# A hybrid decoder layer's opening: rows, first projections, two gates and operand sums emitted in an order that an event simulation of four engines finds

## The chip, the cores and the metric

The kernel runs on one core of one Trainium2 chip. A core has TensorE (PE, matrix products), VectorE (DVE), ScalarE (ACT), GpSimd (POOL) and SyncE (SP, which only issues transfers here); each takes its own instructions in order and waits on semaphores for the others. The metric is the device time of one execution in microseconds (us); lower is better.

## The reference

The whole is one decoder layer in float32 on 1024 tokens of width 1024. What the change touches is the first part, up to the projections:

```
h    = rms_norm(x, norm1_g)              # per token: x * rsqrt(mean(x*x) + 1e-6) * g
proj = h @ w_in + b_in                   # 1024 x D_IN, split by columns into
# qa ka va fa | qb kb vb | qc kc vc ksl vsl kwn vwn gc | gates (3 x 1024)
y_a = fox_attention(qa, ka, va, fa)      # c = cumsum(log_sigmoid(fa)) forgets along the keys
y_b = dilated_attention(qb, kb, vb)
y_c = nsa_attention(qc, ..., gc)
merged = sum(sigmoid(gates[:, i]) * (y_i @ w_i))
x = x + merged @ w_o;  x = x + conv_ffn(rms_norm(x, norm2_g));  return rms_norm(x, final_g)
```

The order in which the parts of `proj` are computed is free. The attention, the merge and the feed-forward part follow on the same core.

## The kernel before

**Numbers.** Every large product is made of three: an operand is split into a rounded high part (ACT, a cast or copy) and a low part, the difference (DVE or POOL, a subtraction with two inputs in SBUF). `mm3` (L294 to L299) issues high x high, high x low, low x high. So each weight and each activation costs one ACT and one DVE or POOL instruction before PE can use it.

**Rows.** `start` (L337 on) loads the eight 128-token rows of x and, after the second, the first token weights. `phase0` (L424) takes row by row: mean square (ACT), a Newton step for the inverse root on DVE (`rstd`, L314 to L324), the scaling x (L428, DVE), two times four transposes by PE into the banks T and S (L433), then the high part hTh (ACT, L436) and the low part hTl (DVE, L437). `constants2` transposes biases and converts masks.

**First tokens.** `proj_va` multiplies each of the eight token blocks with 260 columns (va and fa): 24 matmuls of 260 columns into one of two banks dn. The evacuation tm (L692, DVE) adds the bias and frees the bank; fa (L714) is copied out; v is cast by ACT (L703), its low part made by POOL (L704), and stored. The weights' split bh, bl comes in four chunks (L668 on ACT, L669 on POOL), and the raw chunks go through two buffers wr, so that the third load waits for the first split.

**Gates.** `gate(0)` and `gate(1)` each make two products of 24 matmuls of 512 columns, one per half of the tokens, also into the banks dn. Their weights wl are split by POOL, one instruction of 1024 elements (L275). The evacuation f is an ACT instruction (L1441) and frees the bank, and the result dg is stored from ACT's queue.

**Second tokens.** `proj_vn` does with 274 columns what `proj_va` does with 260, its weights split by POOL (L669).

**Sums.** `token_sums` (L471 on) prepares the operands of a Strassen-like scheme for the later pair products: for each of four slices i it forms T1 (three DVE additions, L488 to L490), T2 (two, L493 and L494), T3 (two, L497 and L498) and T4 (two on POOL, L499 and L501), and splits each (ACT L485; the low part, L486, of T1 and T3 on DVE, of T2 and T4 on POOL). Its steps stand between the tokens and the gates in the program (`step`).

**Decays and first pair.** `fox_decay` takes Exp and Ln of fa (L743, L744 on ACT, with a table load each, after DVE's fax, L741 and L742), sums on DVE and closes with two small products. `proj_pairs` prepares two pair weights before the second tokens (L600 on ACT, L601 on DVE) and starts with pair products of twelve 512-column matmuls; the sums of its weights, su first (L591 to L597), are POOL's. The loads dax, day and dac that the attention needs are issued by POOL behind the last token split.

**What sets the order.** All of this opening is written in program order, and a tile scheduler places each instruction on its engine by its own estimate of when operands come. The attention stage is different: there the class `Flow` simulates the four engines as queues with written costs, and the code is emitted in the order that this simulation finds, under a manual schedule for PE, DVE and ACT. `Flow` holds that a DVE instruction marked `*` and a POOL instruction exclude each other (`self.port`).

Of the kernel before, what the change touches and what calls it, by code (L numbers as in the profile page):

```python
# [141 lines left out]
class Flow:  # L142
# [5 lines left out]
    RATE = 200.0  # L148

    def __init__(self):  # L150
# [3 lines left out]
        r = lambda *names: Ring(self, names)  # L154
        self.S, self.PV = r("S0", "S1"), r("PV")

        self.T = self.dn = r("X0", "X1", "X2")
        self.p, self.th, self.y, self.ce = r(*(f"p{i}" for i in range(6))), r(*range(4)), r(*(f"y{i}" for i in range(8))), r(0, 1)
        self.f, self.groups, self.turned = r("f0", "f1"), r(), r()
# [40 lines left out]
    def move(self, kb):  # L200

        self.moved = max(self.moved, self.now) + kb / self.RATE
# [30 lines left out]
class Trunk:  # L233
    def __init__(self, tc, a, taps=None):
# [4 lines left out]
        self.psA, self.steps = None, None  # L239
# [97 lines left out]
    def start(self):  # L337
# [8 lines left out]
        self.early = Pool(self, "early", {"tm": 2}, side="right")  # L346
        self.hT = [(self.hp.tile([P, 8, 512], F32R, f"hTh{i}"), self.hp.tile([P, 8, 512], F32R, f"hTl{i}")) for i in range(2)]
        self.ident = cp.tile([P, P], F32, "ident")
        xp = self.xp = Pool(self, "x0", {"x": 8, "st": 8, "junk": 2})
        one = xp.tile([P, 1], F32, "one")  # L350
        nc.vector.memset(one, 1.0)
        nc.scalar.activation(one, one, AF.Sqrt)
        self.gb1 = xp.tile([P, D], F32, "gb")
        self.xt = []
        for t in range(NT):
            xt = xp.tile([P, D], F32, "x")
            nc.sync.dma_start(xt, a["x"][0, t * P:(t + 1) * P, :])
            self.xt.append(xt)
            if t == 0:
                nc.scalar.dma_start(self.gb1, a["norm1_g"][0:1].to_broadcast([P, D]))  # L360
                nc.sync.dma_start(self.ident, a["c_main"][:, 0:128])
            if t == 1:
                self.va = self.tok_weights([(C_VA, 260)], 260)
# [16 lines left out]
    def constants2(self):  # L380
        nc, tc, a = self.nc, self.tc, self.a
        cp = self.cp
        t = self.nsac.tile
        c1 = Pool(self, "c1", {})
        if True:
            self.cols = cp.tile([P, 44], F32, "cols")
            rows1 = c1.tile([64, P], F32, "rows1")
            b = a["b_in"][0]
            for r0, o, n in ((0, 0, 4), (4, C_QB, 9), (13, C_QC, 6), (19, C_KWN, 1), (20, C_G, 24)):
                nc.sync.dma_start(rows1[r0:r0 + n], b[o:o + n * P].rearrange("(r p) -> r p", p=P))  # L390
            ps = self.psA.tile([P, 512], F32, "T")
            nc.tensor.transpose(ps[:, 0:44], rows1[0:44], self.ident[0:44, 0:44])
            nc.vector.tensor_copy(self.cols, ps[:, 0:44])
            rows2 = c1.tile([96, P], F32, "rows2")
            nc.sync.dma_start(rows2[0:66], a["conv_w"][0].rearrange("w (r p) -> (w r) p", p=P))
            nc.sync.dma_start(rows2[66:88], a["conv_b"][0].rearrange("(r p) -> r p", p=P))
            pe = c1.tile([32, P], F32, "pe")
            nc.sync.dma_start(pe[:, 0:64], a["cmp_pe"][0])
            nc.sync.dma_start(pe[:, 64:128], a["cmp_pe"][0])
            cm2 = c1.tile([P, 640], F32, "cm2")  # L400
            nc.sync.dma_start(cm2, a["c_main"][:, 384:1024])
            ps = self.psA.tile([P, 512], F32, "T")
            nc.tensor.transpose(ps[:, 0:88], rows2[0:88], self.ident[0:88, 0:88])
            nc.tensor.transpose(ps[:, 128:160], pe, self.ident[0:32, 0:32])
            self.ccols = cp.tile([P, 88], F32, "ccols")
            nc.vector.tensor_copy(self.ccols, ps[:, 0:88])
            self.peT = t([P, 32], F32, "peT")
            nc.vector.tensor_copy(self.peT, ps[:, 128:160])
            mk = t([P, 640], BF16, "mk")
            nc.vector.tensor_copy(mk, cm2)  # L410
        c1.close()
        self.mC, self.mB, self.mW, self.m2, self.mcmp = (mk[:, i * P:(i + 1) * P] for i in range(5))
        self.identb = t([P, P], BF16, "identb")
        nc.vector.tensor_copy(self.identb, self.ident)
        self.sab = t([P, 4, 2, 16], F32, "sab")
        nc.sync.dma_start(self.sab, a["c_sab"].rearrange("p (i s j) -> p i s j", i=4, s=2))
        self.gsig = t([P, NT, 18], F32, "gsig")

        self.k1c = t([P, 256], F32R, "k1c")
        self.k2c = t([98, 256], F32R, "k2c")  # L420
        self.vcs = {(g, pos): t([P, P], F32R, f"vcs{g}{pos}") for g in range(2) for pos in range(2)}


# [130 lines left out]
    def proj_pairs(self, B):  # L554
# [54 lines left out]
        for x in range(2):  # L609
            prep(*seq[x])  # L610
# [1498 lines left out]
```

## Time and profile before

| what | us |
|---|---|
| median of three runs | 1720.72 (1717.38 to 1721.79) |
| the profiled execution | 1718.86 |
| its span, first to last instruction | 1717.0 |
| PE busy in the span | 1651.3 |
| first pair's first product, from the span's start | 114.26 |
| mean granted clock of PE | 0.995 |

The profile is one execution. A start is given from the span's beginning. Busy time of PE counts a matmul until its modelled end, and matmuls overlap, so the price of a matmul is the distance to the next one's start. "Idle before, ended by" names the instruction whose semaphore came last.

### The profile page before, as it was taken

To read this page: it belongs to the slowest core of one execution; us is meant where nothing else is said; L and a number is where in the kernel's file an instruction comes from. 1 tells how busy PE (TensorE), PEld (TensorE's weight loads), DVE (VectorE), ACT (ScalarE), POOL (GpSimd) and SP (SyncE) were. 2 spreads that over 40 slices of the span, in tenths; PEclk is the share of its full clock that TensorE was granted. 3 is DMA by queue.
4 is the path that set the end of the run, shared out by engine and by line. 5 is a ranking of instruction groups with operands and counts; after the bars stand their busy time and mean duration, and the time that the engine had idled before them with its cause. 6 is when DMAs were issued, how large, how long until landed. Compare 5 with 4: busy or idle time off the path is not lost.

```text
span 1717.0 us, 24504 instructions
## 1 busy us (share of the span) xinstructions
PE 1651.3 (96%) x8456; PEld 1367.6 (80%) x8456; DVE 1312.1 (76%) x2234; ACT 837.5 (49%) x1611; POOL 477.3 (28%) x367
## 2 busy tenths in 40 slices
PE   6799999999999999999999999899999999999998
PEld 6688888877888888878776788688888878888876
DVE  8946777554888889898476437999999999866764
ACT  5323453223878877788555314333334333454451
POOL 3752322321000011100124402655555545100000
PEclk9899999999999999999999999999999999999999
DMA  6445556457457664661476600155445544487661
GB/s 207 127 125 147 147 161 166 134 150 194 122 159 176 167 164 119 171 187 55 147 228 200 242 13 13 59 181 181 168 147 184 182 156 147 157 266 228 213 227 51
DMA packets 226571, 269.11 MB, mean 157 GB/s; under 512 B 21184, under 2 KB 162070, under 8 KB 226238
## 3 DMA queue, kind: packets, MB, share of 16 engines
q1 hardware_dynamic: 223262, 259.52, 50.8%
q10 hardware_dynamic: 2736, 5.24, 0.8%
q0 software_dynamic: 448, 2.78, 0.5%
q8 instruction: 67, 1.10, 0.3%
q14 instruction: 58, 0.48, 0.1%
HBM read 188.26 MB, written 81.93 MB: 157 GB/s over the span
## 4 chain that ended last, share of the span: by engine, by line
PE 51%; DVE 25%; issue 8%; DMA 7%; ACT 4%; POOL 4%; SPq 1%; POOLq 0%; DVEq 0%; ACTq 0%
PE X L1470 5%; PE dn L297 4%; PE dn L298 4%; PE dn L299 4%; DVE t L1744 4%; PE X L919 3%; PE S L298 3%; PE S L299 3%; PE S L297 3%; DVE u L1802 3%; PE T L299 2%; PE T L298 2%; PE T L297 2%; PE PV L966 2%; PE S L821 2%
## 5 line engine op out<-in xcount | busy, mean ns | idle before, releaser
L938 DVE TENSOR_TENSOR tl<-X,th 128x512 fp32r<-128x512 f32 (+2 forms) x202 | 116.8, 585 | 16.3 <-ACT th L935 14.3
L1506 POOL TENSOR_TENSOR wl<-wr,wh 128x256 fp32r<-128x256 f32 x44 | 32.5, 771 | 311.9 <-ACT wh L1501 297.2
L935 ACT CAST th<-X 128x512 fp32r<-128x512 f32 (+2 forms) x202 | 101.8, 507 | 33.0 <-PE X L919 30.2
L1744 DVE SCALAR_TENSOR_TENSOR t<-u,ccols,t 128x511 f32<-128x511 f32 (+1 forms) x88 | 96.7, 1099 | 7.5 <-ACT t L1739 6.4
L845 DVE TENSOR_REDUCE sm<-S 128x1 f32<-128x640 f32 (+7 forms) x128 | 87.5, 711 | 16.0 <-PE S L821 14.9
L919 PE MATMUL X<-ident,p 128*128 128x128 f32 x610 | 97.7, 275 | 1.6 <-DVE tl L938 1.4
L853 ACT ACTIVATE p<-S,sm 128x640 f32<-128x640 f32 (+7 forms) x128 | 90.8, 714 | 14.6 <-DVE sm L845 13.9
L965 PE MATMUL PV<-th,v 128*128 128x256 f32 (+1 forms) x362 | 94.3, 283 | 0.2 <-DVE y L986 0.2
L821 PE MATMUL S<-k,q 98*128 98x128 f32 (+6 forms) x240 | 89.5, 381 | 1.5 <-issue 1.5
L966 PE MATMUL PV<-tl,v 128*128 128x256 f32 (+1 forms) x362 | 89.5, 281 | 1.2 <-DVE tl L938 1.2
L817 PE MATMUL S<-k,q 128*128 128x512 f32 (+2 forms) x240 | 81.8, 341 | 2.0 <-ACT p L853 2.0
L275 POOL TENSOR_TENSOR wl<-wr,wh 128x384 fp32r<-128x384 f32 (+2 forms) x31 | 42.8, 1383 | 135.3 <-ACT wh L273 107.8
L919 PEld LDWEIGHTS X<-ident,p 128*128 128x128 f32 x610 | 69.9, 140 | 9.8 <-DVE tl L938 1.7
L297 PE MATMUL dn<-hTh,wh 128*128 128x512 f32 x152 | 61.0, 402 | 12.8 <-ACT f L1441 11.0
L1470 PE MATMUL X<-hTh,wh 128*128 128x512 f32 x176 | 73.1, 415 | 0.0
L966 PEld LDWEIGHTS PV<-tl,v 128*128 128x128 f32 x362 | 68.5, 189 | 5.8 <-DVE tl L938 2.8
L1470 PE MATMUL X<-hTh,wl 128*128 128x512 f32 x176 | 72.6, 413 | 0.0
L965 PEld LDWEIGHTS PV<-th,v 128*128 128x128 f32 x362 | 68.5, 189 | 4.8 <-DVE y L986 2.3
L1669 POOL TENSOR_TENSOR su<-wr 128x512 f32<-128x512 f32 x20 | 31.5, 1576 | 144.9 <-DMA wr<-w_up 72.1
L1470 PE MATMUL X<-hTl,wh 128*128 128x512 f32 x176 | 71.8, 408 | 0.0
L1745 ACT ACTIVATE t<-t 128x512 f32<-128x512 f32 x44 | 27.9, 633 | 83.3 <-DVE t L1744 83.3
L1739 ACT ACTIVATE t<-u,ccols 128x512 f32<-128x512 f32 x44 | 36.0, 817 | 52.2 <-DVE u L1802 49.0
(821 smaller groups left out, 5620.7 us busy)
## 6 DMA issues: line engine op xcount, KB each, us to landing
wr<-w_up SPq DMA_DIRECT2D x66, 256.0 KB
gr<-dg SPq DMA_DIRECT2D x24, 512.0 KB
t<-w_down SPq DMA_DIRECT2D x22, 512.0 KB
dt<-t SPq DMA_DIRECT2D x22, 512.0 KB
wr<-w_in SPq DMA_DIRECT2D x40, 256.0 KB
wr<-dl SPq DMA_DIRECT2D x39, 256.0 KB
wr<-w_in SPq DMA_DIRECT2D x18, 512.0 KB
x<-x SPq DMA_DIRECT2D x16, 512.0 KB
```

The source lines that it names most:

```text
L297: nc.tensor.matmul(out, st[0], mv[0], start=first, stop=False)
L298: nc.tensor.matmul(out, st[0], mv[1], start=False, stop=False)
L299: nc.tensor.matmul(out, st[1], mv[0], start=False, stop=last)
L821: nc.tensor.matmul(out, q.t[1][0:R, qs], k.t[1][0:R, cs], start=False, stop=True)
L853: nc.scalar.activation(o.rearrange("p a b -> p (a b)"), u, AF.Exp, bias=mx[:, x:x + 1], accum_out=sm[:, 2 + x:3 + x])
L919: nc.tensor.transpose(ps[:, n * P:(n + 1) * P], b(), self.ident)
L935: nc.scalar.copy(g.th[:, cs], ps[:, cs])
L938: yield "DVE", 0, 0.07 + cs.stop * 1.04e-3, lambda: nc.vector.tensor_tensor(g.tl[:, cs], ps[:, cs], g.th[:, cs].bitcast(F32), ALU.subtract)
L965: nc.tensor.matmul(unit.pv[:, oc], w, g.th[:, cs], start=first and i == 0, stop=False)
L966: nc.tensor.matmul(unit.pv[:, oc], w, g.tl[:, cs], start=False, stop=e)
L1470: nc.tensor.matmul(p, w[i][:, k], self.hT[hh][j][:, k], start=x == 0, stop=x == 23)
L1744: nc.vector.scalar_tensor_tensor(o, i, cw[2 - sh], o, ALU.mult, ALU.add)
```

## The change

`start`'s loads, `phase0`, `constants2`, `proj_va`, two gates, `tok_weights`, `token_sums` and `proj_vn` are replaced by one function, `opening`. It runs a `Flow` with its own rings of buffers, and each piece of work is a process that asks for an engine at a priority level with a written cost. The order of PE, DVE, ACT and SP is then the simulation's; POOL is still placed by the tile scheduler.

- The first four weight chunks go into four buffers (wr, wr, wh, wl) and are all loaded before the fourth row of x; the second bias has a buffer of its own.
- Low parts of splits (`either`) go to DVE or POOL, whichever is free first in the simulation: for the weights, the gates' weights (in four pieces of 256), the tokens' v and all T1 to T4. T4's two additions may go to either engine too.
- The rows' root is taken by ACT with scale and offset, without waiting for DVE's first step.
- The two gates go side by side: both first halves, then both second halves, with a token block between.
- The gates' stores dg go to SP's queue. The bias transposes use the bank PV and the decays' small products too.
- `Flow.run` gets a rule, which also holds for the attention stage: an instruction that needs the port on DVE is held back while POOL is free and has an older or more urgent one waiting.

```diff
+                held = self.port > self.now + 1e-9
+
+                other = min((o[:2] for o in self.queues["POOL"] if not o[6]), default=None)
+                if e == "DVE" and other and self.free["POOL"] <= self.now + 1e-9:
+                    mine = min((o[:2] for o in q if not o[6] and o[7]), default=other)
+                    held = held or other[0] < mine[0]
-                ready = [o for o in q if not o[6] and not (o[7] and self.port > self.now + 1e-9)]
+                ready = [o for o in q if not o[6] and not (o[7] and held)]
...
+        self.F = F = Flow(250.0, T=range(2), S=range(3), dn=range(2), PV=range(1), tm=range(2), v4=range(2), wr=range(2))
...
+        raws = [raw_chunk(VA, k, t) for k, t in ((0, "wr"), (1, "wr"))]
+        F.wr.names.clear()
+        x(2)
+        raws += [raw_chunk(VA, k, t) for k, t in ((2, "wh"), (3, "wl"))]
...
+        either = lambda level, n, fn: [("DVE*", level, 0.1 + n * 1.04e-3, lambda: fn(v)), ("POOL", level, 0.25 + n * 2.12e-3, lambda: fn(g))]
...
+            yield "DVE", 0, 0.55, biased
+            F.dn.give(bank)
+            place = yield F.v4
+            vs = self.st.tile([P, 4, P], F32R, "v4")
+            tv = tm[:, 0:256].rearrange("p (h d) -> p h d", h=4)
+            yield "ACT", 1, 0.35, lambda: nc.scalar.copy(vs[:, :, 0:64], tv)
+            yield either(1, 256, lambda e: e(vs[:, :, 64:128], tv, vs[:, :, 0:64].bitcast(F32), ALU.subtract))
...
+            w = [wp.tile([P, 8, P], F32R, n) for n in ("wh", "wl")]
+            yield "ACT", 2, 1.0, lambda: nc.scalar.copy(w[0], raw)
+            for k in range(0, 8, 2):
+                yield either(2, 256, lambda e, k=k: e(w[1][:, k:k + 2], raw[:, k:k + 2], w[0][:, k:k + 2].bitcast(F32), ALU.subtract))
...
+            gt = yield "ACT", 0, 0.6, out
+            F.dn.give(bank)
+            yield 0.1
+            nc.sync.dma_start(self.dg[f][:, hh * 512:hh * 512 + 512], gt)
...
+            yield "DVE*", 3, 1.24, third
+            F.proc(split("T3"))
+            yield [("DVE*", 3, 1.24, lambda: fourth(v)), ("POOL", 3, 2.7, lambda: fourth(g))]
...
+        yield "ACT", 3, 3.0, log
...
+        with self.tc.manual_schedule(engines={en.PE, en.DVE, en.Activation, en.SP}):
+            for t in range(NT):
+                F.proc(row(t))
...
-        self.phase0()
-        self.constants2()
-        tp = Pool(self, "sums", {})
-        B = {}
-        self.steps = self.token_sums(tp, B)
+        self.opening()
...
-        self.proj_va()
-        self.gate(0)
-        vn = self.tok_weights([(C_VSL, 128), (C_VWN, 146)], 274)
-        self.gate(1)
```

What it moves, on PE where the last row is transposed (x_126 before and x_140 now are that row; dn_553 is the fifth token block, dn_491 the fifth and dn_540 the sixth). Before:

```order
L299 MATMUL dn_553<-bh_96,hTl_4_81 128x260
L297 MATMUL dn_553<-bh_96,hTh_3_80 128x260
L433 MATMUL T_346<-ident_82,x_126 128x128 x4
L433 MATMUL S_353<-ident_82,x_126 128x128 x4
L298 MATMUL dn_553<-bl_97,hTh_3_80 128x260
```

and now:

```order
L300 MATMUL dn_491<-bh_172,hTl_4_81 128x260
L298 MATMUL dn_540<-bh_172,hTh_3_80 128x260
...
L300 MATMUL dn_540<-bh_172,hTl_4_81 128x260
L459 MATMUL T_552<-ident_82,x_140 128x128 x4
L459 MATMUL S_558<-ident_82,x_140 128x128 x4
L298 MATMUL dn_540<-bh_172,hTh_3_80 128x260
```

Ahead of the last row's transposes stood 109 token matmuls (four blocks of 24 and 13), and now 129 (five blocks and 9).

On ACT around the two table loads of the decays (f with dn are the four gate evacuations: f_157_733 and f_159_773 are those of the first gate before, f_170_837 and f_174_880 of the second; f_171_865 and f_174_908 now are the two second halves). Before:

```order
L485 CAST T2h_472<-sh_775 128x512
L743 ACT_TABLE_LOAD
L743 ACTIVATE fax_1178<-fax_1178 128x32
L485 CAST T3h_474<-sl_776 128x512
L744 ACT_TABLE_LOAD
L744 ACTIVATE flf_1179<-fax_1178,cm_1176 128x32
L600 CAST wh_901<-wr_895 128x512
L485 CAST T3h_474<-f_149_690 128x512
L485 CAST T4h_476<-f_149_690 128x512
L1441 ACTIVATE f_159_773<-dn_748,cols_364 128x512
L485 CAST T4h_476<-sl_776 128x512
```

and now:

```order
L552 ACTIVATE f_171_865<-dn_778,cols_370 128x512
L618 CAST T2h_616<-sh_815 128x512
L958 ACT_TABLE_LOAD
L958 ACTIVATE fax_836<-fax_836 128x32
L959 ACT_TABLE_LOAD
L959 ACTIVATE flf_837<-fax_836,cm_801 128x32
L552 ACTIVATE f_174_908<-dn_791,cols_370 128x512
L618 CAST T3h_618<-sl_869 128x512
```

Before, three of the four gate evacuations stood behind both loads and behind T4h, whose input is POOL's; now one does, and nothing of POOL's stands between.

On POOL at the end of the second tokens (v are the tokens' low parts, su the first pair's first sum). Before:

```order
L704 TENSOR_TENSOR v_194_1068<-tm_1065,v_194_1068 128x4x64
L704 TENSOR_TENSOR v_197_1101<-tm_1098,v_197_1101 128x4x64
L704 TENSOR_TENSOR v_200_1134<-tm_1131,v_200_1134 128x4x64
L704 TENSOR_TENSOR v_203_1167<-tm_1164,v_203_1167 128x4x64
L591 TENSOR_TENSOR su_1225<-wr_896 128x512
```

and now:

```order
L619 TENSOR_TENSOR T1l_615<-sh_913,T1h_614 128x512
L2190 DMA dax_16_96<-c_ax 16x3200
...
L619 TENSOR_TENSOR T3l_619<-sl_1053,T3h_618 128x512
L2192 DMA dac_100<-c_ac 16x800
L878 TENSOR_TENSOR su_1231<-wr_852 128x512
```

All of the second tokens' v stand on DVE now. Over the opening POOL has lost 13 of its 16 sums operations, 4 of 8 weight chunks, 11 of 16 v and a quarter of the gates' splits (2 of 8 pieces), and DVE has them. From the first pair on PE has the same order as before for 3264 rows, which ends in the attention stage, about 671 us into the profile; there some 950 rows stand in another order.

## Rows read from the trace of the kernel before

**Rows 1.** The page: the span, and in part 2 PE's busy tenths in 40 slices of 42.9 us.

```profile
span 1717.0 us, 24504 instructions
...
PE   6799999999999999999999999899999999999998
```

**Rows 2.** Busy time by stretch of the opening, us (from:to, length, then PE, PEld, DVE, ACT and POOL with their counts, the granted clock as a share of full speed, DMA share, GB/s).

```profile
10.00:40.00 30.00, 24.96 (x170) 23.30 (x171) 28.37 (x63) 19.35 (x42) 16.09 (x10) 1.00 0.63 200
40.00:62.40 22.40, 22.35 (x139) 19.74 (x137) 22.10 (x32) 7.28 (x15) 13.88 (x10) 1.00 0.33 90
62.40:98.30 35.90, 23.02 (x121) 19.92 (x121) 29.34 (x37) 13.91 (x24) 27.44 (x26) 0.86 0.47 135
```

**Rows 3.** The timeline of PE in the gates, the second token stage and the first pair (start, duration, line, operation, tile and operands, shape; in brackets PE's idle time before it and what ended it). Matmuls overlap, so the distance between two starts is the price of one.

```profile
63.43 0.50 PE L297 MATMUL dn<-hTh,wh 128*128 128x512 f32 x1 [1.07 <-ACT f L1441]
...
78.74 0.80 PE L297 MATMUL dn<-hTh,wh 128*128 128x512 f32 x1 [9.57 <-ACT f L1441]
...
83.92 0.39 PE L297 MATMUL dn<-hTh,wh 128*128 128x512 f32 x1
...
86.64 0.29 PE L297 MATMUL dn<-bh,hTh 128*128 128x274 f32 x1
...
98.24 0.39 PE L297 MATMUL dn<-bh,hTh 128*128 128x274 f32 x1 [2.28 <-DVE tm L692]
...
114.26 0.50 PE L297 MATMUL dn<-hTh,wh 128*128 128x512 f32 x1
...
120.50 0.50 PE L297 MATMUL T<-T2h,wh 128*128 128x512 f32 x1 [0.51 <-ACT wh L600]
...
127.21 0.39 PE L297 MATMUL dn<-T4h,wh 128*128 128x512 f32 x1
```

**Rows 4.** The same view of PE among the first token products, which share the stage with the rows' transposes.

```profile
35.91 0.36 PE L297 MATMUL dn<-bh,hTh 128*128 128x260 f32 x1 [1.10 <-DVE tm L692]
...
39.91 0.60 PE L433 MATMUL S<-ident,x 128*128 128x128 f32 x4
...
40.59 0.28 PE L297 MATMUL dn<-bh,hTh 128*128 128x260 f32 x1
40.71 0.28 PE L298 MATMUL dn<-bl,hTh 128*128 128x260 f32 x1
```

**Rows 5.** The timeline of ACT around the two table loads and the third gate evacuation (L1441).

```profile
67.11 1.28 ACT L743 ACT_TABLE_LOAD   x1
69.62 0.23 ACT L743 ACTIVATE fax<-fax 128x32 f32<-128x32 f32 x1 [1.23 <-DVE fax L742]
...
71.97 1.28 ACT L744 ACT_TABLE_LOAD   x1
73.27 0.32 ACT L744 ACTIVATE flf<-fax,cm 128x32 f32<-128x32 f32 x1
...
77.48 0.62 ACT L485 CAST T4h<-f 128x512 fp32r<-128x512 f32 x1 [2.18 <-POOL f L501]
78.00 0.68 ACT L1441 ACTIVATE f<-dn,cols 128x512 f32<-128x512 f32 x1
```

**Rows 6.** The timeline of DVE, then of POOL: two-input operations on 128x512.

```profile
61.51 0.68 DVE L493 TENSOR_TENSOR sh<-hTh,sh 128x512 f32<-128x512 f32 x1
62.11 0.68 DVE L493 TENSOR_TENSOR f<-hTh,f 128x512 f32<-128x512 f32 x1
...
71.23 1.75 DVE L497 TENSOR_TENSOR f<-f,hTh 128x512 f32<-128x512 f32 x1
...
70.70 1.72 POOL L499 TENSOR_TENSOR sl<-hTh,sh 128x512 f32<-128x512 f32 x1
72.39 1.71 POOL L499 TENSOR_TENSOR f<-hTh,f 128x512 f32<-128x512 f32 x1
```

**Rows 7.** The timeline of DVE just before the second token's evacuation tm.

```profile
96.49 1.35 DVE L486 TENSOR_TENSOR T3l<-f,T3h 128x512 fp32r<-128x512 f32 x1 [3.04 <-ACT T3h L485]
97.76 0.43 DVE L692 TENSOR_TENSOR tm<-dn,bb 128x274 f32<-128x274 f32 x1
```

**Rows 8.** Lines of DVE between 40 and 98 us (busy time, mean ns of one): five of the 128x512 groups of the sums.

```profile
L486 DVE TENSOR_TENSOR T3l<-sl,T3h 128x512 fp32r<-128x512 f32 x2 | 3.5, 1730 | 0.0
...
L489 DVE TENSOR_TENSOR f<-f,hTl 128x512 f32<-128x512 f32 x2 | 2.6, 1278 | 0.0
...
L494 DVE TENSOR_TENSOR f<-f,hTl 128x512 f32<-128x512 f32 x2 | 2.5, 1267 | 0.0
...
L488 DVE TENSOR_TENSOR sh<-hTh,hTh 128x512 f32<-128x512 f32 x2 | 2.5, 1228 | 0.0
L497 DVE TENSOR_TENSOR f<-f,hTh 128x512 f32<-128x512 f32 x2 | 2.4, 1220 | 0.6 <-DMA dg<-f 0.6
```

**Rows 9.** Busy time in the stretch from 10 to 95 us, columns as in the second group.

```profile
10.00:95.00 85.00, 69.31 (x421) 62.16 (x422) 78.03 (x127) 39.32 (x77) 54.91 (x43) 0.94 0.49 146
```

**Rows 10.** The end of the second token stage on POOL (v is the last token's split, su the first sum of the first pair's weights).

```profile
115.00 0.80 POOL L704 TENSOR_TENSOR v<-tm,v 128x256 fp32r<-128x256 f32 x1 [2.48 <-ACT v L703]
115.77 1.28 POOL L591 TENSOR_TENSOR su<-wr 128x512 f32<-128x512 f32 x1
```

**Rows 11.** Busy time by stretch late in the attention stage, columns as in the second group.

```profile
760.00:780.00 20.00, 18.43 (x126) 15.12 (x125) 18.60 (x41) 16.57 (x41) 2.96 (x4) 1.00 0.54 158
...
820.00:840.00 20.00, 18.15 (x114) 15.59 (x113) 7.68 (x15) 8.68 (x17) 1.42 (x1) 1.00 0.09 28
```

More of the change, by code (lines that the diff above doesn't have):

```diff
@@ L153, in __init__ @@
         self.free = dict.fromkeys(self.queues, 0.0)
[L154 to L159, printed above, removed]
+        for n, names in rings.items():
+            setattr(self, n, Ring(self, names))
     def at(self, t, fn):
@@ L200, in move @@
     def move(self, kb):
-        self.moved = max(self.moved, self.now) + kb / self.RATE
+        self.moved = max(self.moved, self.now) + kb / self.rate
         return self.moved + 2.0 - self.now
@@ L607, in proj_pairs @@
         seq = [(s, i) for s in range(last + 1) for i in range(7)]
-        for x in range(2):
-            prep(*seq[x])
+        yield
+        prep(*seq[0])
+        yield
+        prep(*seq[1])
         pool = yield
@@ new lines, in size, with log, sums @@
+        def size():
+            nc.vector.tensor_scalar(ax, fa, -1.0, None, ALU.mult)
+            nc.vector.tensor_tensor(ax, ax, fa, ALU.max)
+        yield "DVE*", 3, 0.4, size
+        def log():
+            nc.scalar.activation(ax, ax, AF.Exp, scale=-1.0)
+            nc.scalar.activation(lf, ax, AF.Ln, bias=ones[:, 0:1])
+        yield "ACT", 3, 3.0, log
+        def sums():
+            nc.vector.tensor_scalar(mn, fa, 0.0, None, ALU.min)
+            nc.vector.tensor_tensor(lf, mn, lf, ALU.subtract)
+            nc.vector.memset(lp[:, :, 0:1], 0.0)
+            for i in range(1, NT):
+                nc.vector.tensor_tensor(lp[:, :, i], lp[:, :, i - 1], lf[:, :, i - 1], ALU.add)
@@ new lines, in fox_decay, with product @@
+        yield "DVE*", 3, 1.8, sums
+        bank = yield F.PV
+        def product():
+            ps = self.psA.tile([P, 512], F32, "PV")
+            nc.tensor.matmul(ps[0:32, 0:P], lf.rearrange("p h i -> p (h i)"), tri, start=True, stop=False)
+            nc.tensor.matmul(ps[0:32, 0:P], lp.rearrange("p h i -> p (h i)"), ones, start=False, stop=True)
+            return ps
+        ps = yield "PE", 0, 0.6, product
+        cc = self.fcc = self.nsac.tile([32, 4, P], F32R, "fcc")
+        yield "ACT", 3, 0.2, lambda: nc.scalar.copy(cc[:, 0], ps[0:32, 0:P])
@@ L761, in load_q, with rest @@
+        def rest():
+            nc.vector.tensor_tensor(cc[:, 1], ps[0:32, 0:P], cc[:, 0].bitcast(F32), ALU.subtract)
+            nc.vector.tensor_scalar(cc[:, 2], cc[:, 0].bitcast(F32), -1.0, None, ALU.mult)
+            nc.vector.tensor_scalar(cc[:, 3], cc[:, 1].bitcast(F32), -1.0, None, ALU.mult)
+        yield "DVE*", 3, 0.6, rest
+        F.PV.give(bank)
     def load_q(self, dq, h, ax=None, sel=True):
@@ L1517, in weight_list @@
         w = lambda c, sc=None: ([win[:, c:c + P]], 8, P, sc)
-        out = [w(C_G), w(C_G + P), w(C_KC), w(C_VC)] + [w(C_G + f * P) for f in range(2, self.PAIRED)]
+        out = [w(C_KC), w(C_VC)] + [w(C_G + f * P) for f in range(2, self.PAIRED)]
         return out
@@ L1993, in run @@
         self.psum_pool(True)
-        self.F = F = Flow()
+        self.F = F = Flow(200.0, S=("S0", "S1"), T=("X0", "X1", "X2"), PV=("PV",), p=[f"p{i}" for i in range(6)],
+                          th=range(4), y=[f"y{i}" for i in range(8)], ce=range(2), f=("f0", "f1"), groups=(), turned=())
+        F.dn = F.T
         main = self.attention()
```

515 lines of the change are left out of this document (313 added, 202 removed).

## The prediction

> **What bounds the kernel now.** I read the page first: over the span PE is the engine that sets the time, and its busy tenths are 9 nearly everywhere except in the first two slices, which hold a 6 and a 7 [rows 1]. What the change can give is therefore PE's idle and slow time up to the first pair, and nothing that happens to DVE, ACT or POOL counts unless PE waits for it. Next I read the opening by stretches [rows 2]: from 40 to 62.4 us PE is busy 22.35 of 22.40 us; from 62.4 to 98.3 only 23.02 of 35.90 and at a mean granted clock of 0.86; from 10 to 40 it misses 5.04. PE's timeline gives the stalls one by one [rows 3], ACT's and DVE's say why [rows 5, 7].
>
> **The stalls of before.** The third and fourth gate halves need a bank that an ACT evacuation frees. The second evacuation stands in ACT's order behind Exp, Ln, their table loads (1.28 us each), a wait of 1.23 us for DVE's fax and one of 2.18 us for POOL's half of T4 [rows 5]; PE stands 9.57 us. After it the clock is at its lower level: the twelve matmuls from 78.74 to 83.92 take 5.18 us, the twelve from 83.92 to 86.64 take 2.72 [rows 3], so 2.46 are lost to the clock that the idle time cost. Before that, 1.07 us go to the evacuation at 63.43. In the second tokens 2.28 us go to a tm [rows 3], which stood behind a T3 split that had itself idled DVE 3.04 us for ACT [rows 7]. In the first pair four products of twelve matmuls should take 4 x 2.72 = 10.88 us and take from 114.26 to 127.21, 12.95 [rows 3]: 2.07 lost while POOL's sums of the weights, ACT's cast and DVE's split follow each other. Behind 127.21 PE does not wait again for the opening. The sum is 1.07 + 9.57 + 2.46 + 2.28 + 2.07 = **17.45 us**.
>
> **Term 1, these stalls.** The new ACT order has two evacuations before the loads; one stands behind them with nothing of POOL's between. That one frees the bank that the second token of the next stage needs: one token block is 24 matmuls of 274 columns, by columns 274/260 of the 0.12 of [rows 4] each (an estimate), about 3.0 us in all, so this evacuation has 3.0 us after its product's end. What must follow the product in that time is one evacuation, 0.68 [rows 5], and, if ACT is only then at the loads, two loads and two ACTIVATEs, 2 x 1.28 + 0.23 + 0.32: 3.8 in all [rows 5]. It fits if DVE's fax comes a microsecond before the product ends, and I take it as hidden, since the two halves of the gates before it last 2 x 2 x 2.72 = 10.9 us and the loads can begin within the second. The second load ended at 71.97 + 1.28 = 73.25 and the ACTIVATE behind it began at 73.27 [rows 5], so a load costs its own time and no more here.
>
> The Trainium skill (ScalarE: Activation LUTs, section "What ACT_TABLE_LOAD costs") puts a drain of about 1.38 us beside each load's 1.28. By it two switches would cost 2.8 us more, the evacuation would be hidden only if fax came nearly four microseconds before the product's end, and otherwise up to 2.8 of the 17.45 would stay; the rows show no such gap, and the sum goes by the rows.
>
> With PE not standing, the clock loss goes too. The tm stall goes because DVE no longer waits for POOL's T4 there: T4's additions are now DVE's own. So −17.45.
>
> **Term 2, the rows.** PE has 129 token matmuls ahead of the last row's transposes instead of 109. The transposes come when DVE has scaled that row; I take the same 40 us [rows 4], because DVE does the same seven steps for it (it loses one small step a row and gains v and bl splits). Twenty matmuls at 0.12 (40.59 to 40.71) [rows 4] are then done earlier: −2.4. Bounds: 0, if the extra splits delay DVE, and −5.0, all that PE misses in that stretch [rows 2].
>
> **Term 3, the first pair.** su began at 115.77, when POOL had done the last v, 0.80 us that itself began after ACT's cast [rows 10]. Now it needs only the tm before it and comes about 1.4 us earlier, so of the 2.07 about 0.7 stay: +0.7 (bounds 0 and 2.07).
>
> **Term 4, what DVE now carries.** Moved to it are 13 sums operations of 128x512 at 0.60 (61.51 to 62.11) [rows 6], four weight chunks at about 0.62 and eleven v and two gate pieces of half the width at about 0.30 (estimates, by columns): 7.8 + 2.5 + 3.9 = **14.2 us**. Between 10 and 95 us DVE was busy 78.03 of 85.00 [rows 9]; 78.0 + 14.2 = 92.2 would not fit. But part of the 78 is collision: beside a POOL operation of 1.72 us DVE's takes 1.75 instead of 0.68 [rows 6], and the five groups of [rows 8] stand, two instructions each, 2 x (1730 + 1278 + 1267 + 1228 + 1220 − 5 x 680) ns = 6.6 us above that. The moved work leaves POOL, so these collisions mostly go: 92.2 − 6.6 = 85.6, in a stretch of 85. That is full, not over, and other collisions that I have not listed go as well. So I expect stalls to appear, small ones, of the kind of 1.10 at 35.91 [rows 4] and 1.07 at 63.43 [rows 3]: **+2.2**; bounds 0 (from 40 to 62.4 PE ran on with DVE busy 22.10 of 22.40 [rows 2]) and 7.2 (92.2 − 85).
>
> **Edits at nothing.** Four buffers for the first chunks: the token products' stalls that I list before 40 us are ended by DVE, as the one at 35.91 [rows 4], not by a chunk; the later rows of x come behind two more chunks and can be late by as much, which lies inside term 2's bounds: 0. dg on SP's queue: SP waits there for f, and behind it stand two of the second tokens' weight chunks, then, for the later pair of stores, the v stores; the chunks are needed a gate half later, which covers them. POOL's dax issues now stand between the last sums splits, with no product waiting on them before the attention. The other order in the attention stage, 950 rows, touches a stretch where PE misses 1.57 + 1.85 = 3.4 us in its two weakest windows [rows 11]: it can win about that and, as an estimate, lose as much: 0, ±3.
>
> **Sum.** −17.45 − 2.4 + 0.7 + 2.2 = **−17.0**. The profiled execution took 1718.86 (span 1717.0 and 1.86 around it) and so would take 1701.9; the median of the runs stands 1.86 above the profiled one, so I forecast **1703.7**.
>
> **Rivals.** (a) *DVE paces the opening.* No collision is won back and the rows gain nothing: −17.45 + 0.7 + 7.2 = −9.6, time 1711. For it: DVE was busy 92% of that stretch already. Against: POOL, which it collided with, loses over half of its two-input work. (b) *The gate stall stays.* DVE reaches fax late, since its order has a unit of sums and a weight chunk ahead of it, the fourth evacuation comes late and the second token stage starts with 9.57 + 2.46 as before: −17.0 + 12.0 = −5.0, time 1716. For it: the evacuation still stands behind both loads. Against: only one does, and it has a token block of time. (c) *Slower: DVE's load stretches under the collisions.* If each moved operation costs k times its own time because it meets POOL's, the overflow is 78.0 + 14.2k − 85; it eats −17.45 − 2.4 + 0.7 = −19.15 from k = 1.84 on, and at k = 1.75/0.60 = 2.9 it is 34 us and the kernel takes about 1736. For it: exactly that ratio stands in [rows 6]. Against: POOL keeps few operations to meet. (d) *The attention order* loses more than the opening's rest wins; inside ±3 it only shifts the forecast.
>
> **Chances.** The forecast, 1698 to 1709: 0.74. (a) 0.13, (b) 0.08, (c) 0.04, and 0.01 for less than all stalls going with a slower attention. The range reaches from 1697 (no new stall, −2.2, and the attention winning 3, with the measurement's spread) to 1713 (a with 2 more). A measurement of this kernel tells about 0.3% from no change, 5.2 us, so faster means under 1715.6: all of the forecast and of (a), and half of (b), 0.90; within 0.06; slower 0.04.
>
> **What would show it.** Right: the first pair's first product at 95 to 98 us, the fifth at 107 to 110; PE idle under 8 us between 10 us and there; no window of clock 0.7 after 20 us; DVE's 128x512 sums near 0.7 us. Wrong: a stall of several us ended by a gate evacuation (b); many stalls ended by tm with DVE full (a, c), with sums operations at 1.2 to 1.75 us (c); a first pair at 95 with a time that is not lower, which would put the loss behind the opening (d).

## The result, and the profile after

| | changed kernel | kernel before |
|---|---|---|
| median, us | 1708.01 (1703.52 to 1708.70, 4 runs) | 1721.26 (1717.38 to 1725.26, 4 runs) |
| ratio, 95% interval | 0.9917 (0.9889 to 0.9946) | |
| profiled execution, us | 1708.70 | 1718.86 |
| first pair's first product | 103.27 | 114.26 |
| its fifth product (T4h), where PE waits no more for the opening | 115.55 | 127.21 |

The kernel is 13 us faster, 0.8%, inside the range and 4.3 us above the forecast of 1703.7. The first pair starts later than the prediction asked for, though, at 103.27 instead of 95 to 98, and the fifth product at 115.55 instead of 107 to 110. The span of the new profile:

```profile
span 1706.6 us, 24506 instructions
```

The stretches of the opening, columns as in [rows 2]:

```profile
10.00:40.00 30.00, 26.48 (x189) 24.84 (x189) 28.72 (x65) 19.93 (x41) 10.70 (x12) 1.00 0.62 199
40.00:62.40 22.40, 22.05 (x132) 19.39 (x131) 21.95 (x45) 9.20 (x17) 2.53 (x2) 1.00 0.30 87
62.40:98.30 35.90, 31.07 (x202) 28.44 (x201) 30.88 (x63) 14.19 (x26) 12.72 (x18) 0.98 0.64 184
```

PE is busy 26.48 of the first 30 us (24.96 before) and 31.07 of the third stretch (23.02 before), at a clock of 0.98 there instead of 0.86; the second is as full as it was. DVE is at 28.72, 21.95 and 30.88, about what it was, and POOL, at 57.41 us between 10 and 98.3 before, has 25.95 (the three numbers summed). What is left is read from PE's timeline, which answers to [rows 3, 4] (columns as there):

```profile
39.98 0.60 PE L459 MATMUL T<-ident,x 128*128 128x128 f32 x4
...
74.84 0.39 PE L298 MATMUL dn<-bh,hTh 128*128 128x274 f32 x1 [0.68 <-ACT f L552]
...
95.56 0.39 PE L298 MATMUL dn<-bh,hTh 128*128 128x274 f32 x1 [4.11 <-DVE tm L507]
...
96.70 0.43 PE L300 MATMUL dn<-bh,hTl 128*128 128x274 f32 x1
...
99.90 0.36 PE L299 MATMUL dn<-bl,hTh 128*128 128x274 f32 x1
...
103.27 0.40 PE L298 MATMUL dn<-hTh,wh 128*128 128x512 f32 x1
...
110.44 0.50 PE L300 MATMUL T<-T2h,wh 128*128 128x512 f32 x1 [0.84 <-DVE wh L888]
...
115.55 0.39 PE L298 MATMUL dn<-T4h,wh 128*128 128x512 f32 x1
```

The last row's transposes begin at 39.98. The gates' wait of 9.57 us is 0.68. A new stall of 4.11 us stands at 95.56, with the clock at its lower level behind it: from 96.70 to 99.90 the granted clock is 0.50, and the 14 matmuls take 3.20 us, 0.229 each, where the estimate for full speed was 0.127. The first pair runs from 103.27 to 115.55.

ACT around the table loads, the counterpart of [rows 5], and one row later:

```profile
70.42 0.61 ACT L618 CAST T2h<-sh 128x512 fp32r<-128x512 f32 x1
71.05 1.28 ACT L958 ACT_TABLE_LOAD   x1
72.35 0.23 ACT L958 ACTIVATE fax<-fax 128x32 f32<-128x32 f32 x1
...
74.12 0.67 ACT L552 ACTIVATE f<-dn,cols 128x512 f32<-128x512 f32 x1
...
91.29 0.40 ACT L515 CAST v<-tm 128x256 fp32r<-128x256 f32 x1 [3.34 <-DMA dv_w<-v]
```

Loads, Exp and Ln follow each other without a wait for fax, and the last gate evacuation begins at 74.12. The last row is the cast of the fourth token block's v, which stood 3.34 us until the buffer was free, that is, until a store dv_w of the second block's v (half of it, 128 KB) had landed. SP had issued that store here (start, duration of the issue):

```profile
84.05 0.46 SPq L519 DMA_DIRECT2D dv_w<-v  x1
```

and DVE, whose order has that v ahead of T2, of T4's additions and of the next evacuation tm, stood with it:

```profile
91.73 0.42 DVE L516 TENSOR_TENSOR v<-tm,v 128x256 fp32r<-128x256 f32 x1 [2.54 <-ACT v L515]
...
92.67 1.75 DVE L636 TENSOR_TENSOR sl<-hTh,sh 128x512 f32<-128x512 f32 x1
...
95.07 0.44 DVE L507 TENSOR_TENSOR tm<-dn,bb 128x274 f32<-128x274 f32 x1
```

So the store of 128 KB takes 7.2 us, from 84.05 to 91.29; then v gets its buffer, DVE goes on 2.54 us late, and PE gets its bank only after tm at 95.07. One addition of T4 took 1.75 us in between. Over the opening DVE's collisions with POOL are few: of the groups of the sums only two stand above a mean of 0.7 us, each by what one instruction of its four takes more. Lines of DVE from 40 to 103 us, as in [rows 8]:

```profile
L629 DVE TENSOR_TENSOR sh<-sh,hTl 128x512 f32<-128x512 f32 x4 | 3.8, 953 | 0.1
L636 DVE TENSOR_TENSOR sl<-hTh,sh 128x512 f32<-128x512 f32 x4 | 3.8, 949 | 0.0
```

### The profile page after: what moved, and what is told of

Read it like the earlier page. It is cut to its first block, busy times and chain, and to the rows that moved or that the text cites. A ratio compares the mean times of both kernels' runs of the same rounds, so it can differ in the third digit from the quotient of the medians.

```text
span 1706.6 us, 24506 instructions
## 1 busy us (share of the span) xinstructions
PE 1650.2 (97%) x8456; PEld 1368.0 (80%) x8456; DVE 1310.2 (77%) x2264; ACT 836.2 (49%) x1612; POOL 440.1 (26%) x343
## 4 chain that ended last, share of the span: by engine, by line
PE 69%; DVE 15%; issue 5%; DMA 5%; ACT 3%; POOL 3%; SPq 0%; POOLq 0%; DVEq 0%; ACTq 0%
PE X L1700 6%; PE dn L298 6%; PE dn L300 6%; PE dn L299 6%; PE S L300 5%; PE S L299 5%; PE S L298 5%; PE X L1150 4%; PE T L300 3%; PE T L299 3%; PE T L298 3%; PE PV L1197 2%; PE S L1052 2%; PE PV L1196 2%; PE S L1048 2%
## 5 line engine op out<-in xcount | busy, mean ns | idle before, releaser
L276 POOL TENSOR_TENSOR wl<-wr,wh 128x384 fp32r<-128x384 f32 (+2 forms) x29 | 38.6, 1335 | 135.4 <-ACT wh L274 105.8
```

## The experiments

A time is a median over the runs of one chip, and a ratio is to the kernel before on the same chip. Where a few microseconds are at issue, the start of the fifth pair product T4h in the profiled execution is the sharper reading (127.21 before, 115.55 in the changed kernel).

### What the stall of 4.11 us is

**A third buffer for v** (v4_three). The Exp of the gate logits writes in place, to make the room; all orders are those of the changed kernel.

```diff
-        self.st = Pool(self, "stage", {"f4": 2, "b8": 2, "v4": 2}, side="right")
+        self.st = Pool(self, "stage", {"f4": 2, "b8": 2, "v4": 3}, side="right")
...
-            e = early.tile([P, NT, 18], F32, "ge")
+            e = gl
```

> Theory S (the store holds the evacuation): in the changed kernel the one stall of 4.11 us at 95.56 comes about because the fourth token's v waits for one of two buffers until a store lands 7 us after its issue, and DVE, whose order has that v ahead of T2, T4 and the next tm, stands with it. With a third buffer for v (the in-place Exp of the gate logits makes the room; the orders of all engines stay) v needs the buffer of three tokens earlier, which has landed: the stall and the 1.6 us of slow clock behind it go, the fifth pair product (T4h) starts at about 110 instead of 115.5, and the time falls by 5 to 6 us to about 1702.5. Rival L (DVE's load and its collisions with POOL's T3 split are late anyway): the stall stays at 3 to 4 us, T4h at 114.5 to 115.5, the time at 1708.

Measured: 1701.26 us, ratio 0.9891 (0.9875 to 0.9908). PE's timeline and DVE's:

```profile
92.93 0.39 PE L298 MATMUL dn<-bh,hTh 128*128 128x274 f32 x1 [1.45 <-DVE tm L507]
...
111.05 0.39 PE L298 MATMUL dn<-T4h,wh 128*128 128x512 f32 x1
```

```profile
89.08 0.42 DVE L516 TENSOR_TENSOR v<-tm,v 128x256 fp32r<-128x256 f32 x1
...
90.02 1.78 DVE L636 TENSOR_TENSOR sl<-hTh,sh 128x512 f32<-128x512 f32 x1
...
92.44 0.44 DVE L507 TENSOR_TENSOR tm<-dn,bb 128x274 f32<-128x274 f32 x1
```

The store no longer counts: v runs at 89.08 without a wait, the granted clock from 90 to 100 us is 1.00 (0.83 in the changed kernel), T4h comes 4.5 us earlier. The stall is 1.45 and not gone; what precedes that tm is T4's addition of 1.78 us.

**The table loads later** (dax_late).

```diff
         with self.tc.issue_after(self.last_split.ins):
-            for i in range(12):
-                nc.gpsimd.dma_start(self.dax[i], a["c_ax"][i])
             nc.gpsimd.dma_start(self.day, a["c_ay"])
...
+                self.last_s4 = g(d["A12"], d["A12"], d["S2"], ALU.subtract)
...
         self.pairs.send(pp)
+        with self.tc.issue_after(self.last_s4.ins):
+            for i in range(12):
+                nc.gpsimd.dma_start(self.dax[i], a["c_ax"][i])
```

> The twelve table loads dax that POOL issues between 69 and 85 us are issued only behind the last pair's weight sums. Theory S1 (these 2.4 MB delay the v stores): the stores land in 3 us or so, two buffers suffice, the stall of 4.11 us shrinks under 1.5 us, T4h starts at 110 to 111.5, the time is about 1703. Rival S2 (two buffers are too few with or without them, since the second tokens' stores are many small packets): the stores still take 5 us and more, at least 2.5 us of the stall stay, and the time is 1706 or more. Rival L as before: stall unchanged, 1708.

Measured: 1703.73 us, ratio 0.9902 (0.9879 to 0.9925). PE, then ACT:

```profile
93.14 0.40 PE L298 MATMUL dn<-bh,hTh 128*128 128x274 f32 x1 [1.51 <-DVE tm L507]
...
111.67 0.39 PE L298 MATMUL dn<-T4h,wh 128*128 128x512 f32 x1
```

```profile
88.05 0.40 ACT L515 CAST v<-tm 128x256 fp32r<-128x256 f32 x1
```

With two buffers still, v is cast at 88.05 without a wait, 3.8 us after that same store's issue at 84.25 in this run, so the store had landed by then: it took 7.2 us because 2.4 MB of tables were on their way at the same time. From 84 to 91.3 us the DMA engines are busy 0.74 of the time in the changed kernel and 0.34 here. Either cure does nearly the same, S and S1 hold, L falls; S1's figures are missed narrowly (a stall under 1.5, T4h by 111.5).

**The second tokens' split on POOL** (vn_split_on_pool).

```diff
-            yield either(1, 256, lambda e: e(vs[:, :, 64:128], tv, vs[:, :, 0:64].bitcast(F32), ALU.subtract))
+            yield either(1, 256, lambda e: (g if n == 274 else e)(vs[:, :, 64:128], tv, vs[:, :, 0:64].bitcast(F32), ALU.subtract))
```

> The low parts of the second tokens' v go back to POOL, with DVE's other work in the same order. Theory S: nothing of DVE stands behind a store any more, so the stall of 4.11 us and its slow clock go (-5.7), while the first sum of the pair's weights waits for the last v again (+0.8 to 1.3): T4h at 110.5 to 111.5, time about 1703.5. Rival L: DVE is relieved by eight operations of 0.34, 2.7 us in all, of which those before the stall are four, so the stall falls by 1.4 at most: T4h at 114 or later, time 1707.

Measured: 1704.59 us, ratio 0.9908 (0.9893 to 0.9923). PE's timeline:

```profile
93.02 0.39 PE L298 MATMUL dn<-bh,hTh 128*128 128x274 f32 x1 [0.63 <-DVE tm L507]
...
105.87 0.50 PE L298 MATMUL T<-T2h,wh 128*128 128x512 f32 x1 [1.04 <-ACT wh L887]
...
112.59 0.39 PE L298 MATMUL dn<-T4h,wh 128*128 128x512 f32 x1
```

With v off DVE nothing of DVE stands behind a store, and the stall is 0.63. The last v on POOL brings back 1.04 us at the pair's weights (0.51 in [rows 3]), and the decays' product waits 1.07 us for DVE's flp at 78.78, which it did not in the changed kernel. T4h is 3.0 us earlier than there, not 4 to 5 as expected.

### What the attention stage has to do with it

**The old rule there** (old_rule_attention), and **the new rule alone** in the kernel before (before_new_rule).

```diff
-        self.rate = rate
+        self.rate, self.hold = rate, True
...
-                if e == "DVE" and other and self.free["POOL"] <= self.now + 1e-9:
+                if self.hold and e == "DVE" and other and self.free["POOL"] <= self.now + 1e-9:
...
+        F.dn, F.hold = F.T, False
```

```diff
+                held = self.port > self.now + 1e-9
+                other = min((o[:2] for o in self.queues["POOL"] if not o[6]), default=None)
+                if e == "DVE" and other and self.free["POOL"] <= self.now + 1e-9:
+                    mine = min((o[:2] for o in q if not o[6] and o[7]), default=other)
+                    held = held or other[0] < mine[0]
-                ready = [o for o in q if not o[6] and not (o[7] and self.port > self.now + 1e-9)]
+                ready = [o for o in q if not o[6] and not (o[7] and held)]
```

> The new rule of the simulation holds in the opening only; the attention stage gets the order of the kernel before. Theory R (the lag of the changed kernel behind the earlier one falls by 4 to 6 us over the rows with another order, so the new order is worth that): the opening is unchanged, with T4h at 115.5, and the time is 4 to 6 us higher, 1712 to 1714. Rival N (the two orders are worth the same, and what the lag shows there is waiting that merely moved): within 2 us of 1708.

> Kernel before, with the simulation's new rule in its attention stage and nothing else. Theory R (the new order there is worth 4 us, as taking it out of the changed kernel cost): 1716 to 1717. Rival T (it is worth something only from the changed start, since the order depends on the loads that are under way): within 1.5 us of before.

Measured: without the rule 1712.23 us, ratio 0.9952 (0.9936 to 0.9967), against 0.9917 with it; with the rule alone 1715.94, ratio 0.9962 (0.9946 to 0.9978). What PE waited for from 660 to 845 us (us in total, times, longest), first without the rule, then in the changed kernel:

```profile
PE dn L298 <- ACT f L1713: 1.6, 1, 1.6
PE X L1150 <- DVE tl L1169: 1.1, 2, 0.8
PE PV L1197 <- DVE tl L1169: 1.0, 3, 0.5
```

```profile
PE PV L1197 <- DVE tl L1169: 0.2, 1, 0.2
```

The waits of 1.6 us for an evacuation and of 2.1 us for splits are gone with the new order; the kernel before with the rule has the same 0.2 left. Theory R holds on both sides: N and T fall. The order is worth about 6 us by the ratios and 3 by the ends of the profiled executions.

### Where the opening's gain comes from

**All splits on their old engines** (splits_fixed): the choice of engine is no longer the simulation's, the order still is. It is not the changed kernel's order, since the simulation runs anew.

```diff
-            out = yield [o for o in either(1, 2 * n, low) if not last or o[0] == "POOL"]
+            out = yield [o for o in either(1, 2 * n, low) if o[0] == "POOL"]
...
-            yield either(1, 256, lambda e: e(vs[:, :, 64:128], tv, vs[:, :, 0:64].bitcast(F32), ALU.subtract))
+            yield either(1, 256, lambda e: e(vs[:, :, 64:128], tv, vs[:, :, 0:64].bitcast(F32), ALU.subtract))[1]
...
-                yield either(2, 256, lambda e, k=k: e(w[1][:, k:k + 2], raw[:, k:k + 2], w[0][:, k:k + 2].bitcast(F32), ALU.subtract))
+                yield either(2, 256, lambda e, k=k: e(w[1][:, k:k + 2], raw[:, k:k + 2], w[0][:, k:k + 2].bitcast(F32), ALU.subtract))[1]
...
-                yield either(3, 512, lambda e: e(B[n][1][:, i], r[n], f[n][0], sub))
+                yield either(3, 512, lambda e: e(B[n][1][:, i], r[n], f[n][0], sub))[n in ("T2", "T4")]
...
-            yield [("DVE*", 3, 1.24, lambda: fourth(v)), ("POOL", 3, 2.7, lambda: fourth(g))]
+            yield "POOL", 3, 2.7, lambda: fourth(g)
```

**Only the sums on theirs** (sums_fixed): the last two of these edits.

> Changed kernel in which each split stays on the engine that it had before (weights, gates' weights, v, T2 and T4 with T4's additions on POOL; T1 and T3 on DVE), and the simulation orders the rest. Theory E (the freedom of the splits is worth a good part, since POOL with 57 us of work beside DVE's cannot be done with the sums in time): the sums' last T4 on POOL ends only shortly before the first pair's weight sums, DVE's two-input operations take 1.2 us and more beside it, T4h starts at 118 or later, and the time is 1711 or more. Rival O (the order and the gates' evacuations are all of it): T4h at 116 or earlier, time 1704 to 1709.

> Changed kernel in which only the sums' low parts and T4's additions stay on the engine that they had before (T2, T4 on POOL); weights, gates' weights and v stay free. Theory P (with all splits fixed the opening lost its whole gain because POOL's sums stand ahead of the first pair's weight sums): T4h starts at 121 or later, time 1714 or more. Rival V (it was the v and the weight chunks on POOL): T4h at 117 or earlier, time 1710 or less.

Measured: splits_fixed 1723.24 us, ratio 1.0001 (0.9988 to 1.0014); sums_fixed 1709.49, ratio 0.9924 (0.9903 to 0.9945). POOL and PE at the first pair, splits_fixed:

```profile
113.52 1.26 POOL L619 TENSOR_TENSOR T4l<-sl,T4h 128x512 fp32r<-128x512 f32 x1
114.75 1.71 POOL L878 TENSOR_TENSOR su<-wr 128x512 f32<-128x512 f32 x1
```

```profile
118.50 0.80 PE L298 MATMUL S<-T3h,wl 128*128 128x512 f32 x1 [8.45 <-ACT wl L887]
...
127.03 0.39 PE L298 MATMUL dn<-T4h,wh 128*128 128x512 f32 x1
```

and sums_fixed:

```profile
101.37 1.29 POOL L619 TENSOR_TENSOR T4l<-sl,T4h 128x512 fp32r<-128x512 f32 x1 [2.83 <-ACT T4h L618]
102.62 1.55 POOL L878 TENSOR_TENSOR su<-wr 128x512 f32<-128x512 f32 x1
```

```profile
100.32 0.47 PE L298 MATMUL dn<-hTh,wh 128*128 128x512 f32 x1 [0.54 <-DVE tm L507]
...
115.76 0.39 PE L298 MATMUL dn<-T4h,wh 128*128 128x512 f32 x1
```

With everything fixed the gates' wait is 2.64 us instead of 9.57, but POOL's last sums end at 114.8, su starts there, and the first pair stands 8.45 us for a weight: T4h is at 127.03, as before the change. Behind it, 3.9 us lost from 418 to 421 (the wait of the section on the bank and slow clock behind it) cancel the attention rule's gain. So the order alone gave nothing up to T4h (E holds, O falls).

With the sums fixed and weights and v free, the last T4 ends at 102.6 and T4h is at 115.76, so P's figures fall and V's come. But the sums on POOL are not free. No cast of v waits for a store in this run, and the pair starts 2.95 us earlier than in the changed kernel; it then takes 15.44 us instead of 12.28, with 2.03 us of waits for the splits of its weights and a granted clock of 0.62 from 109 to 112. Against v4_three, where no store counts either, T4h is 4.7 us later.

Nor are the second tokens' v what POOL had to be rid of: with these on POOL and the rest free (vn_split_on_pool) T4h is at 112.59. Either part alone can go back to POOL and leave most of the gain; everything together cannot. These runs suggest that POOL's work as a whole counts. How it divides they do not show: the sums free, with all weights and v fixed, was not tried.

**The decays later in the kernel before** (before_decay_late).

```diff
-                nc.scalar.activation(gt, ps, AF.Identity, bias=self.cols[:, 20 + f:21 + f])
+                self.gate_evac = nc.scalar.activation(gt, ps, AF.Identity, bias=self.cols[:, 20 + f:21 + f])
...
+        with self.tc.issue_after(self.gate_evac.ins):
+            nc.scalar.activation(ax, ax, AF.Exp, scale=-1.0)
```

> Kernel before, with the decays' Exp and Ln and their two table loads behind the fourth gate evacuation. Theory G (the loads, the wait for fax and POOL's T4 ahead of the second evacuation are the stall of 9.57 us): the second evacuation moves up by 5 us or more, the stall falls to 3 to 5 us, the slow clock behind it goes at least in part, and the time is 6 to 8 us lower, 1712 to 1715. Rival P (POOL and DVE, busy 97% there, are the pace, and the stall comes back a little later in the second tokens): T4h not earlier than 125, the time within 2 us of before.

Measured: 1716.21 us, ratio 0.9968 (0.9956 to 0.9980). ACT, then PE:

```profile
74.20 0.69 ACT L1442 ACTIVATE f<-dn,cols 128x512 f32<-128x512 f32 x1 [1.66 <-POOL f L499]
```

```profile
74.94 0.80 PE L297 MATMUL dn<-hTh,wh 128*128 128x512 f32 x1 [5.87 <-ACT f L1442]
...
86.83 0.39 PE L297 MATMUL dn<-bh,hTh 128*128 128x274 f32 x1 [1.54 <-ACT f L1442]
...
95.53 0.60 PE L297 MATMUL dn<-bh,hTh 128*128 128x274 f32 x1 [2.33 <-DVE tm L692]
...
125.90 0.39 PE L297 MATMUL dn<-T4h,wh 128*128 128x512 f32 x1
```

The second evacuation comes at 74.20 instead of 78.00, behind a wait of 1.66 us for POOL now; the stall is 5.87 instead of 9.57. But 1.54 us appear at the next stage, 2.33 stay, and T4h gains 1.3 only. In the time the gain is 3.4 to 7.6 us by the interval; the profiled execution is the slowest of this run's ten. Neither theory holds whole: the stall falls by 3.7 us to 5.87, where G expected 3 to 5 to be left, and P has T4h's place (125 or later) but not the time. How much the moved loads are worth stays open between 1.3 and 7.6.

### A wait behind the opening

In the changed kernel the first fill product X of the attention waited, where the one before ran on (PE, changed kernel, then before):

```profile
409.13 0.47 PE L1700 MATMUL X<-hTh,wh 128*128 128x512 f32 x1 [2.13 <-DVE vcs L1551]
```

```profile
418.34 0.48 PE L1470 MATMUL X<-hTh,wh 128*128 128x512 f32 x1
```

**The decays' product in T** (decay_in_T).

```diff
-            ps = self.psA.tile([P, 512], F32, "PV")
+            ps = self.psA.tile([P, 512], F32, "T")
```

> Changed kernel, with the decays' small product in a bank T again, as before, instead of PV; nothing else. In the changed kernel the first fill product X of the attention, at 409, waits 2.13 us for DVE's vcs copies, where the kernel before ran on. Theory B (banks T are two, taken in turn; the kernel before took eleven of them ahead of the pairs and the changed one takes eight, so that the last one of the compression falls on the bank that X needs first): with nine the turn is as before, the wait goes, with 2.1 to 2.5 us of lag and the slow clock that some runs show behind it, and the time is 1704 to 1706. Rival W (vcs comes late for X because of the earlier start, whichever bank): the wait stays, 1708.

Measured: 1705.42 us, ratio 0.9900 (0.9878 to 0.9922). PE:

```profile
407.62 0.48 PE L1700 MATMUL X<-hTh,wh 128*128 128x512 f32 x1
```

The wait is gone. The product ahead of X starts 0.81 us later than in the changed kernel and X 1.51 earlier, so 2.3 us are won at this place: B holds, W falls. The intervals of the two times overlap; the trace shows it.

### Together

**The third buffer and the late loads** (v4_three_dax_late), **with the product in T** (all_three), and **with the last T3 split on DVE** (all_three_t3):

```diff
-                yield either(3, 512, lambda e: e(B[n][1][:, i], r[n], f[n][0], sub))
+                yield either(3, 512, lambda e: (v if i == 3 else e)(B[n][1][:, i], r[n], f[n][0], sub))
```

> Third buffer for v and the twelve table loads behind the pairs, together. Theory S: both take away the same wait, so they do not add: the stall before the fourth token stays at the 1.5 us that DVE's T4 addition of 1.75 beside POOL's T3 split leaves, T4h starts at 110.5 to 111.5, and the time is 1700 to 1702. Rival A (the loads cost something else as well, in the transfers of the weights or the pairs): the time is 1698 or less, with the gain behind the first pair.

> Third buffer for v, table loads behind the pairs, the decays' product in T. Each takes away a wait of its own place: 1699.8 for the first two, less 2.1 to 3.5 for the third by theory B: 1696 to 1698; by rival W 1700.

> The same, with the last slice's T3 split on DVE, so that no two-input operation of POOL stands beside DVE's T4 addition. Theory C (the 1.4 us that are left of the stall are that collision, 1.75 instead of 0.69): the stall falls to 0.7 or less, since DVE has 0.6 more of its own, T4h at 110.2 to 110.6, time 0.5 to 1 us under that of the kernel without it. Rival L (DVE is late by its load): stall and time as without it.

Measured: 1699.78 us, ratio 0.9868 (0.9845 to 0.9891); 1698.79, 0.9866 (0.9847 to 0.9886); **1696.87, 0.9856 (0.9837 to 0.9875)**. The first two cures do not add, as S says (T4h at 111.13, against 111.05 with the buffer alone). The product in T moves the time by 1.0, where 2.1 or more were expected, and the two intervals overlap almost wholly: in the time its gain is not shown here. With T3's split on DVE, T4's addition, PE's waits from 40 to 125 us, and T4h:

```profile
89.55 0.68 DVE L636 TENSOR_TENSOR sl<-hTh,sh 128x512 f32<-128x512 f32 x1
```

```profile
PE T L300 <- DVE wh L888: 0.7, 1, 0.7
PE dn L298 <- ACT f L552: 0.7, 1, 0.7
PE dn L298 <- DVE tm L507: 0.4, 1, 0.4
```

```profile
109.58 0.39 PE L298 MATMUL dn<-T4h,wh 128*128 128x512 f32 x1
```

The addition is back at 0.68, the stall in the second tokens is gone (the 0.4 is the tm at 60), T4h is 1.5 us earlier: C holds. The 1.9 us between the medians are within the overlap of the intervals. This last kernel beats the changed one, 0.9875 against 0.9889 at the nearest ends of the intervals.

## Why the prediction was right, and where it was off

**The time came within the range; the opening did not come as forecast.** T4h moved by 11.7 us, where the sum has 17.0; that is nearer to rival (a)'s 9.6. Of the four signs of a right forecast only the sums' 0.69 us came: the pair's products are late, PE is idle 8.7 us between 10 us and the pair (under 8 was asked for), and the granted clock is 0.50 behind the stall. That the time is still only 4.3 us from the forecast is in part luck: what the attention's order won pays for two losses behind the opening that I had not priced (below), and the medians differ by about 3 us more than the two profiled executions in which the opening is read.

**Term 1 (−17.45) was right in size.** Four of its five stalls went, and what is left of the fifth, the pair's, is term 3. The evacuation behind the table loads cost 0.68 us: DVE's fax was there, and load, ACTIVATE, load, ACTIVATE and evacuation took 71.05 to 74.8. The Trainium skill (ScalarE: Activation LUTs, section "What ACT_TABLE_LOAD costs") has a drain of 1.38 us for each switch; here the load begins at 71.05, behind a cast that ended at 71.03, and the ACTIVATE follows at 72.35 a load that ended at 72.33, so the measurement decides against it, as the sum had it. But *why* they went was in part wrong. I gave the gain to ACT's order and to T4's additions on DVE. In the kernel before, the loads moved out of the way took 3.7 us from the stall of 9.57 and 1.3 from T4h; splits_fixed cut that stall to 2.64 by its order and lost all of it in the first pair, behind POOL; and sums_fixed has T4's additions on POOL and T4h where the changed kernel has it. What the gain needs is POOL relieved of enough work; the runs do not show that it must be a certain part.

**Term 2 (−2.4) was nearly right.** The last row's transposes begin at 39.98; before they began at 39.45, one group of four, 0.46 us, ahead of the row at 39.91 in [rows 4]. Twenty more matmuls at 0.12, less 0.5 us: −1.9.

**Term 3 (+0.7) was too small.** The pair takes 115.55 − 103.27 = 12.28 us over 10.88: +1.4, of which 0.84 is DVE's split of a weight.

**Term 4 (+2.2, bounds 0 and 7.2) was mis-sized, and for another reason than its own.** New stalls are 0.35 (a tm at 59.94), 0.68 and 4.11, and 14 matmuls at 0.229 instead of 0.127 lose 1.4: 6.5 in all. DVE's load is not the cause: the sums run at 0.69, and a third buffer takes away 2.7 of the 4.11 and the 1.4 at the same load. The 1.45 that it leaves go with the one collision (all_three_t3). The step that failed stands under the edits at nothing: "POOL's dax issues now stand between the last sums splits, with no product waiting on them before the attention". No product waits for the tables, but their transfers delay the stores of v; and through the move that term 4 priced by its duration alone, v's split to DVE, a store now holds an evacuation. The kernel before had a late store too, issued at 99.87, and its trace shows it (ACT):

```profile
104.04 0.41 ACT L703 CAST v<-tm 128x256 fp32r<-128x256 f32 x1 [4.81 <-DMA dv_w<-v]
```

There it held ACT's cast and behind that POOL's split, and no evacuation: PE did not wait between 98.24 and the pair. The terms as measured, −17.45 − 1.9 + 1.4 + 6.5 = −11.5, meet T4h's −11.7. Without the store and the collision (all_three_t3) T4h moves by 17.6; the forecast had 17.0 for a kernel without these cures.

**Behind the opening** gains and losses nearly cancel. The attention's order I put at 0 ± 3: it gives 3 to 6 us. The bank of the decays' product, which the diff changes and I did not price, costs 2.3 at 409. And between 540 and 600 us another 1.9 are lost: both kernels have a wait of 1.5 us there, with the granted clock at 0.83 behind it in the changed kernel (550 to 560) and at 1.00 before; why is open. In the profiled runs, by the starts of the same products, the changed kernel is 11.7 us ahead at T4h, 7.3 at 600, 11.0 at 900 and 10.4 at the end; the medians differ by 13.3. The profiled run of before lies under its median, that of the changed kernel at the top of its runs, which is most of that difference.

**The rivals.** (a) and (c) did not come by their mechanism: nearly all of DVE's sums are at their own duration, and the 1.75 that PE waited behind is beside POOL's last T3 split. (b) did not come. (d) came with the other sign, and reaches past its ±3.

## What to carry to other kernels

When a step moves to another engine, price what it *waits for* as well as its duration: all that is queued behind it there inherits the wait. Here the old trace showed that wait already, at a place where nothing hung on it. A transfer that nobody needs soon can lengthen one that somebody does, as the tables did the store. Two buffers taken in turn carry a parity: leaving out an odd number of uses shifts which one a later stage meets first, far from the edit.

## What the runs showed that I had not expected

- Two cures of one wait, a buffer more (−4.5 us at T4h) and 2.4 MB of loads later (−3.9), give −4.4 together.
- The simulation's order with the old engines is worth nothing up to T4h (127.03 against 127.21); with the choice free for weights and v alone T4h comes 11.3 us earlier (115.76), though the first pair itself then takes 3.2 us longer, with the sums on POOL.
- A bank's turn is worth 2.3 us at 409 us, over 300 us behind the edit that shifted it.
- Four edits that the profile of the changed kernel suggests bring 11 us more: 1696.87 against 1708.01, each beside its own runs of the kernel before (0.9856 and 0.9917).
